# Layer B attention: where the rounding of the value differences and four output weight loads stand in their queues

## The chip, the core and the metric

The kernel runs on one core of one Trainium2 chip. The metric is the device time of one execution in microseconds (us). A core has a matrix engine, TensorE (PE in the profile; its weight loads are PEld), and three engines for elementwise work: VectorE (DVE), ScalarE (ACT) and GpSimd (POOL). SyncE (SP) issues the DMAs. Each engine works through its own list of instructions in order; semaphores hold an instruction back until what it needs is there. GpSimd does not touch the accumulator memory (PSUM) in this kernel; the other three do.

## The reference

A two-layer decoder trunk over one sequence of 2048 tokens of width 1024, in float32. Layer A is a causal attention with a forget gate over 16 heads of 64. Then keys and values for layer B are projected once for 4 shared heads. Layer B, which the change touches, is a sliding-window attention (window 128) in blocks of 128 queries; four query heads share one key/value head, and each head has a learned sink logit:

```
logits = einsum(q, k_band) * 64**-0.5          # k_band: the block before and the block's own keys
logits = where(in_window & valid, logits, -inf)
probs = softmax(concat([logits, sink]))[..., :-1]
out = einsum(probs, v_band)
h = h + (out * silu(gate)) @ w_out_b
```

## The kernel before

Every float32 operand of a matrix product is kept as a rounded high part and a remainder (tiles with `h` and `l`, or two halves of one tile), and a product is the sum of three or four matmuls of such parts.

The program is written with a framework that records operations and schedules them: it decides for each engine in which order its instructions stand, by dependencies and its own estimates. `self.tc.keep_in_program_order(ins)` pins an instruction behind the one that was recorded before it on the same engine, so that the scheduler cannot move it ahead.

Layer B's attention is the generator `attention_b` (L1308 on). Its units are the 64 pairs (block i of 16, key/value head g of 4). Step n of its loop does, in the order of the code:

- `scores(n)` (L1354 to L1373): eight matmuls into a PSUM tile, the mask (L1366), the sink (L1367) and the row maximum (L1370) on DVE, the exponentials on ACT (L1373, four of them, each followed by the read-out of its sum).
- `norm_weights(n-1)`: a reciprocal on DVE (L1382) and a product on POOL (L1383).
- `feed`: some matmuls of the output projection `project` (L1498), the filler between the parts of a step. A step gets 12 of them, in two groups of six. Two steps fill one PSUM bank (tag `pb`, one buffer), which DVE empties at the end (L1504) into the tile with the residual; SP then stores it (L1505).
- at n = 4i + 1, `differences(i)`: on POOL the value tile of block i less that of block i-1 (L1412), then high and low halves of the difference added (L1413).
- `weights_t(n-3)`: transposes on PE (L359), the high part on ACT (L1398), the remainder on DVE (L1399), and on POOL both times the triangle mask (L1402).
- `values(n-4)`: four matmuls (L1437), two with the values of block i-1 and two with the differences, a copy on ACT (L1444), two adds (L1447) and the gate (L1451) on DVE, and the result's high part on ACT (L1453) and remainder on DVE (L1454).
- at n = 4i + 2, `split_differences(i)`: the sum rounded on ACT (L1420), and the remainder as a last subtraction on POOL (L1421). The matmuls of step 4i + 4 and the three after it read the pair.
- loads for the next block on SP: queries and keys (L1327, L1328, L1331), values (L1340) and gates (L1344). L1331, for one, loads the keys' second copy, `big<-kb`.
- `weight_load(j)` for the numbers j in `B_WEIGHTS_AT[n]` (L85): 1 MB of the split output weights, `big<-wo` (L1476). Numbers 4 to 7 are read first by the projection in steps 10 and 11; two of them fill one tile, and the last tile comes free when earlier transposes are done with it.

Until step 7 the attention runs between the matmuls of the gate projection (L742); from step 8 on, the output projection fills. Steps then follow each other on PE without other work.

Of the kernel before, what the change touches and what calls it, by code (L numbers as in the profile page):

```python
# [18 lines left out]
ALU = mybir.AluOpType  # L19
# [10 lines left out]
HD = 64  # L30
# [51 lines left out]
B_AHEAD = 8  # L82
B_LOAD_AT = 6

B_WEIGHTS_AT = {4: (0,), 5: (1,), 6: (2,), 7: (3,), 8: (4, 5), 9: (6, 7)}  # L85
FEED_1 = 0
FEED_2 = 6

# [12 lines left out]
def f_(ap):  # L101
    return ap.bitcast(F32)
# [51 lines left out]
class Trunk:  # L154
# [1153 lines left out]
    def attention_b(self, res, dst):  # L1308

        nc, d = self.nc, self.d  # L1310
# [25 lines left out]
        def load_v(i):  # L1336

            ts_ = slice(i * P, (i + 1) * P)
            v = self.sb(("qn", "qn", "wr")[i % 3], [P, NKV, P], F32R)
            nc.sync.dma_start(  # L1340
                out=f_(v), in_=d["vb"][:, ts_, :].rearrange("g t e -> t g e")
            )
            g = yg[:, 2 + i % 2, :].rearrange("p (c t) -> p c t", t=P)
            nc.sync.dma_start(out=g, in_=d["gtb"][:, ts_].rearrange("(c p) t -> p c t", p=P))  # L1344
            blk[i][3:5] = v, g
# [70 lines left out]
        def split_differences(i):  # L1416

            t_ = dvs[i][:, :, :HD]
            dv = self.sb("wh", [P, NKV, P], F32R)
            nc.scalar.copy(dv[:, :, :HD], t_)  # L1420
            nc.gpsimd.tensor_tensor(dv[:, :, HD:], t_, f_(dv[:, :, :HD]), ALU.subtract)  # L1421
            dvs[i] = dv

        def values(u):
# [47 lines left out]
        def weight_load(j):  # L1472
            half, t = 1 - j // 4, j % 4 * 2
            if t % 4 == 0:
                W[half][t // 4] = self.sb("big", [P, 2, 4, CH], F32R)
            nc.sync.dma_start(  # L1476
                out=f_(W[half][t // 4][:, :, t % 4 : t % 4 + 2, :]),
                in_=d["wo"][half, t // 4, :, :, t % 4 : t % 4 + 2, :],
            )
# [37 lines left out]
        for n in range(N + V_LAG_B):  # L1517
            if n < N:
                scores(n)
            if 0 < n <= N:  # L1520
                norm_weights(n - 1)
            if n == T_LAG_B:
                php = self.sb("big", [P, 2, 2, 2, G, P], F32R)
            if n == V_LAG_B + NKV:
                odd += [[self.sb(t, [P, 4, P], F32R) for _ in range(2)] for t in ("wh", "wl")]
            o = (n - O_LAG_B) * per
            feed(o + FEED_1)
            if n % NKV == 1 and NKV < n < N:
                differences(n // NKV)
            if 0 <= n - T_LAG_B < N:  # L1530
                weights_t(n - T_LAG_B)
            feed(o + FEED_2)
            if 0 <= n - V_LAG_B < N:
                values(n - V_LAG_B)
            if n % NKV == 2 and NKV < n < N:
                split_differences(n // NKV)
            feed(o + per)
            if n < N:
                i, g = units[n]
                if g == NKV - 2 and i + 1 < NTB:  # L1540
                    load(i + 1)
                if g == NKV - 1 and i + 1 < NTB:
                    load_v(i + 1)
            for j in B_WEIGHTS_AT.get(n, ()):
                weight_load(j)
            yield
# [123 lines left out]
```

## Time and profile before

| what | before |
|---|---|
| median of 3 timed runs | 2434.48 us (2434.19 to 2435.48) |
| the profiled execution, its own time | 2432.39 us |
| its span, first to last instruction | 2430.3 us |
| granted TensorE clock over the span | 1.000 |
| busy in the span: PE, DVE, ACT, POOL | 99%, 71%, 52%, 41% |
| DMA | 436.04 MB, mean 179 GB/s |

In the rows of the profile, `L1420 ACT` is line 1420 on ScalarE, and `out<-in` names the tiles by the program's own names. A row of the waits says whose instruction stood idle for whom: total us, how often, the longest. In a timeline a row has its start, its length and, in brackets, the idle time just before it and who ended that. A row of windows has the stretch, its length, the busy us of PE, PEld, DVE, ACT and POOL, the clock, the busy share of the 16 DMA engines and GB/s. Starts are from the span's start; layer B's attention fills the stretch from some 2040 us to the end, with the output projection in it from 2109 us.

### The profile page before, as it was taken

Reading aid. Unit: us, or ns where it says so; the run is one execution under the profiler, and the core shown is the slowest. Engines: PE = TensorE matmul, PEld = TensorE weight load, DVE = VectorE, ACT = ScalarE, POOL = GpSimd, SP = SyncE. Lnnn points to the kernel's source line nnn. Section 1 sums busy time; section 2 is a strip of 40 time slices with the busy share of each in tenths; the row PEclk is TensorE's granted clock in tenths of the full one; section 3 lists DMA queues with packets and bytes.
Section 4 is the critical chain, followed back from the end, with each engine's and each line's share of the span. In section 5 each row is a group of like instructions: output and inputs, shape, how many; then the busy total and the mean of one; then the engine's idle time right before and its main releaser. Section 6 shows DMA issues by size and latency. Waiting matters only on the chain.

```text
span 2430.3 us, 36305 instructions
## 1 busy us (share of the span) xinstructions
PE 2405.9 (99%) x11960; PEld 2025.9 (83%) x11960; DVE 1729.5 (71%) x4086; ACT 1261.7 (52%) x2504; POOL 993.9 (41%) x642
## 2 busy tenths in 40 slices
PE   9999999999999999999999999999999999999999
PEld 7888899987888788888888878888888888888887
DVE  7656567735988888889988865556766543677775
ACT  5433324323878777777877761135323322455554
POOL 0000000011878777777878862200011000377775
PEclk9999999999999999999999999999999999999999
DMA  6656545677554655575466549965433574765552
GB/s 191 201 168 194 154 148 172 197 234 234 176 165 127 207 159 145 148 219 169 130 193 172 172 144 316 294 234 161 126 100 108 167 244 150 257 189 179 181 178 74
DMA packets 356989, 436.04 MB, mean 179 GB/s; under 512 B 65280, under 2 KB 248608, under 8 KB 350624
## 3 DMA queue, kind: packets, MB, share of 16 engines
q1 hardware_dynamic: 356800, 433.71, 59.0%
q8 instruction: 95, 1.56, 0.3%
q14 instruction: 94, 0.77, 0.1%
HBM read 273.69 MB, written 159.79 MB: 178 GB/s over the span
## 4 chain that ended last, share of the span: by engine, by line
PE 89%; DMA 4%; DVE 3%; ACT 2%; issue 1%; POOL 1%; SPq 0%; DVEq 0%; ACTq 0%; POOLq 0%
PE b L779 30%; PE pa L1044 10%; PE pb L1086 7%; PE pb L1498 5%; PE b L1271 5%; PE sc L1000 5%; PE sc L1001 5%; PE mx L955 5%; PE pb L742 3%; PE b L742 2%; PE pa L1437 2%; PE b L1354 2%; DMA wr<-wg 2%; PE pb L359 1%; PE pa L742 1%
## 5 line engine op out<-in xcount | busy, mean ns | idle before, releaser
L779 PE MATMUL b<-wh,big 128*128 128x512 f32 (+3 forms) x2560 | 771.4, 374 | 1.7 <-ACT wh L502 1.4
L1020 POOL TENSOR_TENSOR big<-st,big 128x1024 fp32r<-128x1024 f32 (+1 forms) x320 | 656.0, 2069 | 239.9 <-ACT big L1019 159.4
L779 PEld LDWEIGHTS b<-wh,big 128*128 128x128 f32 x2560 | 470.7, 188 | 73.5 <-ACT wh L502 3.9
L779 PE MATMUL b<-wl,big 128*128 128x512 f32 (+3 forms) x1280 | 473.6, 370 | 1.1 <-DVE wl L503 1.1
L1029 DVE TENSOR_TENSOR ac<-ac,st 128x512 f32<-128x512 f32 (+3 forms) x576 | 352.8, 612 | 52.1 <-ACT st L1016 26.6
L1016 ACT ACTIVATE st<-sc 128x512 f32<-128x512 f32 (+1 forms) x512 | 273.6, 582 | 119.7 <-PE sc L1001 52.3
L1044 PE MATMUL pa<-big 128*128 128x512 f32 (+3 forms) x1280 | 318.9, 365 | 0.6 <-POOL big L1020 0.6
L1019 ACT CAST big<-st 128x1024 fp32r<-128x1024 f32 (+1 forms) x320 | 295.5, 924 | 8.5
L779 PEld LDWEIGHTS b<-wl,big 128*128 128x128 f32 x1280 | 241.3, 189 | 36.8 <-DVE wl L503 4.6
L1044 PEld LDWEIGHTS pa<-big 128*128 128x128 f32 x1280 | 229.1, 190 | 38.8 <-POOL big L1020 2.1
L968 DVE TENSOR_REDUCE mt<-mx 128x1 f32<-128x384 f32 (+1 forms) x360 | 214.5, 598 | 30.4 <-PE mx L955 28.0
L511 ACT ACTIVATE sq<-b,r 128x512 f32<-128x512 f32 (+2 forms) x128 | 77.8, 608 | 302.7 <-PE b L779 302.7
L1000 PE MATMUL sc<-big 128*128 128x512 f32 (+3 forms) x640 | 232.9, 368 | 1.1 <-DVE st L558 1.1
L1001 PE MATMUL sc<-big 67*128 67x512 f32 (+3 forms) x640 | 229.5, 367 | 0.0
L955 PE MATMUL mx<-big 66*128 66x512 f32 (+2 forms) x600 | 225.0, 380 | 0.2
L1086 PE MATMUL pb<-wh,wr 128*128 128x512 f32 x488 | 177.7, 396 | 5.3 <-DMA wr<-wg 5.2
L513 DVE TENSOR_REDUCE sm<-sq 128x8 f32<-128x512 f32 (+2 forms) x128 | 74.8, 584 | 139.7 <-ACT sq L511 139.6
L1402 POOL TENSOR_TENSOR big<-big,tri 128x1024 fp32r<-128x1024 f32 x60 | 143.9, 2399 | 70.2 <-DVE big L1399 70.2
L879 POOL MEMSET rot<- 128x512 bf16 x1 | 0.5, 525 | 418.8 <-PE pb L359 418.8
L963 DVE CUSTOM_DVE_ANT_0 mx<-mx,rot 128x384 f32<-128x384 f32 (+2 forms) x240 | 146.9, 617 | 18.9 <-PE mx L955 17.6
L1000 PEld LDWEIGHTS sc<-big 128*128 128x128 f32 x640 | 121.7, 190 | 22.8 <-DVE st L558 1.5
L1001 PEld LDWEIGHTS sc<-big 67*128 67x128 f32 x640 | 121.8, 190 | 19.3
(285 smaller groups left out, 4122.1 us busy)
## 6 DMA issues: line engine op xcount, KB each, us to landing
wr<-wg SPq DMA_DIRECT2D x62, 512.0 KB, 4.5
va<-st SPq DMA_DIRECT2D x32, 512.0 KB, 4.6
ka<-st SPq DMA_DIRECT2D x64, 256.0 KB, 3.8
ut<-big SPq DMA_DIRECT2D x16, 1024.0 KB, 7.0
big<-ka SPq DMA_DIRECT2D x16, 1024.0 KB
big<-qa SPq DMA_DIRECT2D x16, 1024.0 KB, 8.1
qb<-st SPq DMA_DIRECT2D x64, 256.0 KB, 3.8
big<-qb SPq DMA_DIRECT2D x16, 1024.0 KB, 7.3
```

The source lines that it names most:

```text
L779: nc.tensor.matmul(ps[:, :n], u[tb // 4][:, dt, us], W[k][dt], start=(dt == 0 and i == 0), stop=(dt == NDT - 1 and i == 2),)
L955: mm = nc.tensor.matmul(ps, qb[:66, i * P : (i + 1) * P], kb[:66, k0:k1], start=True, stop=True,)
L963: nc.vector.tensor_tensor_reduce(out=ps, in0=ps, in1=mask_m[:, 512 - w :], scale=1.0, scalar=NEG, op0=ALU.add, op1=ALU.max, accum_out=f_(o),)
L968: nc.vector.reduce_max(o, ps, axis=AX.X)
L1000: nc.tensor.matmul(o, ka[:, ks], qa[:, qs], start=not (last and n_), stop=False)
L1001: nc.tensor.matmul(o, kb[:, ks], qb[:, qs], start=False, stop=not diag)
L1016: nc.scalar.activation(pf[:, off : off + w], ps[:, :w], AF.Exp, scale=HD**-0.5)
L1019: nc.scalar.copy(ph[:, :tw], pf[:, :tw])
L1020: nc.gpsimd.tensor_tensor(pl[:, :tw], pf[:, :tw], f_(ph[:, :tw]), ALU.subtract)
L1029: nc.vector.tensor_tensor(a_, a_, pf[:, off : off + w], ALU.add)
L1044: nc.tensor.matmul(pv[:, q0 : q0 + w], v[:, k, :], src[:, off : off + w], start=(p == 0 and n_ == 0 and i == 0), stop=(last and n_ == 1 an ...
L1086: nc.tensor.matmul(ps, w[:, dt // 2 % 2, wk, dt % 2, :], us[dt][uk], start=(dt == 0 and i == 0), stop=(dt == NDT - 1 and i == 2),)
```

## The change

In `split_differences` both instructions are pinned behind what was recorded before them on their engines, and the weight loads 6 and 7 are issued at step 8, with 4 and 5, instead of step 9.

```diff
-B_WEIGHTS_AT = {4: (0,), 5: (1,), 6: (2,), 7: (3,), 8: (4, 5), 9: (6, 7)}
+B_WEIGHTS_AT = {4: (0,), 5: (1,), 6: (2,), 7: (3,), 8: (4, 5, 6, 7)}
...
             dv = self.sb("wh", [P, NKV, P], F32R)
-            nc.scalar.copy(dv[:, :, :HD], t_)
-            nc.gpsimd.tensor_tensor(dv[:, :, HD:], t_, f_(dv[:, :, :HD]), ALU.subtract)
+            self.tc.keep_in_program_order(nc.scalar.copy(dv[:, :, :HD], t_))
+            self.tc.keep_in_program_order(
+                nc.gpsimd.tensor_tensor(dv[:, :, HD:], t_, f_(dv[:, :, :HD]), ALU.subtract)
+            )
             dvs[i] = dv
```

Behind these lines everything stands two lines lower: L1421 becomes L1422, L1453 becomes L1455, L1476 becomes L1478. The lists of PE and DVE keep their order; those of ACT, POOL and SP change.

On ACT, this stood before around the rounding of block 6 (`wl_22058` is the sum, `wh_22143` the rounded pair; `pa` tiles are units' outputs, `fl` tiles transposes; the time of this place is 2199.66 us in the trace):

```order
L1444 COPY wr_20470<-pa_22020 64x512 [waits PE_49,Activation_49]
L1373 ACTIVATE st_21996,rs_21994<-b2_21982,nm_21993 128x129 [waits DVE_49]
L1373 ACTIVATE st_21996,rs_21994<-b2_21982,nm_21993 128x129 x3
L1420 CAST wh_22143<-wl_22058 128x4x64 [waits Pool_49]
L1453 CAST wh_21073<-pa_22020 128x256 [waits DVE_49]
L1398 CAST big_20722<-fl_22061 128x512 [waits PE_49,Activation_49]
```

and this stands there now:

```order
L1455 CAST wh_21073<-pa_22020 128x256 [waits DVE_49]
L1398 CAST big_20722<-fl_22061 128x512 [waits PE_49,Pool_49]
L1373 ACTIVATE st_22051,rs_22049<-b2_22037,nm_22048 128x129 [waits DVE_49]
L1373 ACTIVATE st_22051,rs_22049<-b2_22037,nm_22048 128x129 x3
L1446 COPY wr_20470<-pa_22075 64x512 [waits PE_49,Activation_49]
L1398 CAST big_20722<-fl_22115 128x512 [waits PE_49,Pool_49]
L1455 CAST wh_21073<-pa_22075 128x256 [waits DVE_49]
L1446 COPY wr_20470<-pa_22132 64x512 [waits PE_49,Activation_49]
L1373 ACTIVATE st_22108,rs_22106<-b2_22094,nm_22105 128x129 [waits DVE_49]
L1373 ACTIVATE st_22108,rs_22106<-b2_22094,nm_22105 128x129 x3
L1455 CAST wh_21074<-pa_22132 128x256 [waits DVE_49]
L1420 CAST wh_22143<-wl_22058 128x4x64 [waits Pool_49]
```

The rounding L1420 has moved from ahead of the high part of `pa_22020` to behind that of `pa_22132`, two steps later (2209.6 us in the trace of before), where L1398 of the next transposes follows it.

On POOL, this stood before around the same block's differences:

```order
L1412 TENSOR_TENSOR wl_22058<-qn_21979,wr_21749 128x512 [waits DMAHW6_49]
L1413 TENSOR_TENSOR wl_22058<-wl_22058 128x4x64 [waits Pool_49]
L1383 TENSOR_TENSOR st_21939<-st_21939,rs_21937 128x4x128 [waits DVE_49]
L1421 TENSOR_TENSOR wh_22143<-wl_22058,wh_22143 128x4x64 [waits Activation_49]
L1402 TENSOR_TENSOR big_20722<-big_20722,tri_110 128x1024 [waits DVE_49]
```

and this stands there now:

```order
L1413 TENSOR_TENSOR wl_22058<-wl_22058 128x4x64 [waits Pool_49]
L1383 TENSOR_TENSOR st_21939<-st_21939,rs_21937 128x4x128 [waits DVE_49]
L1402 TENSOR_TENSOR big_20722<-big_20722,tri_110 128x1024 [waits DVE_49]
L1383 TENSOR_TENSOR st_21996<-st_21996,rs_21994 128x4x128 [waits DVE_49]
L1402 TENSOR_TENSOR big_20722<-big_20722,tri_110 128x1024 [waits DVE_49]
L1383 TENSOR_TENSOR st_22051<-st_22051,rs_22049 128x4x128 [waits DVE_49]
L1422 TENSOR_TENSOR wh_22143<-wl_22058,wh_22143 128x4x64 [waits Activation_49]
L1402 TENSOR_TENSOR big_20722<-big_20722,tri_110 128x1024 [waits DVE_49]
```

The last subtraction has moved past two mask products (L1402) and two weight products (L1383), and stands directly ahead of the third mask product.

On SP, this stood before around the last three of the eight weight loads (`big_21111` is the tile of loads 4 and 5, `big_21171` that of 6 and 7):

```order
L1476 DMA big_21111<-wo_73 128x2x1024 [waits DMAHW2_49]
L1476 DMA big_21171<-wo_73 128x2x1024 [waits DMAHW3_49,PE_49]
L1505 DMA out_h<-sq_21085 128x512 [waits DVE_49]
L1476 DMA big_21171<-wo_73 128x2x1024 [waits DMAHW5_49]
L1493 DMA sq_21203<-h1_68 128x512 [waits DMAHW6_49,DMAHW1_49]
L1331 DMA big_20666<-kb_70 64x4x256 [waits DMAHW7_49]
```

and this stands there now (`big_21114` is the tile of 6 and 7):

```order
L1478 DMA big_21111<-wo_73 128x2x1024 [waits DMAHW2_49]
L1478 DMA big_21114<-wo_73 128x2x1024 [waits DMAHW3_49,PE_49]
L1478 DMA big_21114<-wo_73 128x2x1024
L1507 DMA out_h<-sq_21085 128x512 [waits DMAHW5_49,DVE_49]
L1495 DMA sq_21203<-h1_68 128x512 [waits DMAHW6_49,DMAHW1_49]
L1331 DMA big_20666<-kb_70 64x4x256 [waits DMAHW7_49]
```

Only load 7 changes its place: from behind the first output store to ahead of it. Load 6 still waits for PE, which frees its tile.

## The prediction

> **What bounds the kernel now.** The page comes first. Its first line says that TensorE (PE) is busy nearly always, so a change pays only where PE stands still.
>
> ```profile
> PE 2405.9 (99%) x11960; PEld 2025.9 (83%) x11960; DVE 1729.5 (71%) x4086; ACT 1261.7 (52%) x2504; POOL 993.9 (41%) x642
> ```
>
> Next I read the waits of layer B's attention alone: first PE's own, from 1960 us on; then those of its weight loads (PEld) in the same stretch; then the weight loads between 2200 and 2380 us; then ScalarE's (ACT). Columns: total us, times, longest.
>
> ```profile
> PE pb L1498 <- DVE sq L1504: 2.8, 9, 0.5
> ```
>
> ```profile
> PEld pb L1498 <- DMA big<-wo: 2.1, 2, 1.6
> PEld b L1354 <- DMA big<-kb: 0.5, 1, 0.5
> PEld pa L1437 <- POOL big L1402: 0.3, 1, 0.3
> ```
>
> ```profile
> PEld pb L1498 <- DVE sq L1504: 5.0, 9, 0.7
> ```
>
> ```profile
> ACT wh L1420 <- POOL wl L1413: 21.9, 13, 2.2
> ```
>
> TensorE has three small leaks here. Nine times the output projection (L1498) waits for VectorE to empty its bank (L1504); two of the eight output weight loads come late (wo), and one load of keys (kb); once the values wait for GpSimd. The last row is no wait of TensorE, but it is the change's first target: ACT stands 21.9 us, in 13 places, in front of the rounding of the value differences, L1420.
>
> The rows 2.8 and 5.0 speak of the same nine waits. I take 5.0, because the starts bear it out: in the timeline of weight loads the projection's groups of six start at
>
> ```profile
> 2197.35 1.23 PEld L1498 LDWEIGHTS pb<-big 128*128 128x128 f32 x6
> ...
> 2202.93 1.22 PEld L1498 LDWEIGHTS pb<-big 128*128 128x128 f32 x6 [0.50 <-DVE sq L1504]
> ...
> 2207.98 1.23 PEld L1498 LDWEIGHTS pb<-big 128*128 128x128 f32 x6
> ```
>
> 5.58 us apart with the wait, 5.05 without: 0.53 for one, near 5.0 / 9 = 0.56, where 2.8 / 9 would be 0.31. With 2.8 in place of 5.0 the sum below would come out at 2431.6 us instead of 2429.4. The Trainium skill, page "Perfetto Trace Analysis", section "Identifying the Most-Contended Engine", calls the busy share of matmuls a poor measure, since they are pipelined, and prefers that of weight loads. The trace agrees with the page, by the 0.53.
>
> Is L1420 what makes L1504 late? The timelines of one such unit, POOL, ACT and DVE, show it (brackets: idle before, and who ended it):
>
> ```profile
> 2197.52 1.29 POOL L1412 TENSOR_TENSOR wl<-qn,wr 128x512 f32<-128x512 f32 x1
> 2198.89 0.74 POOL L1413 TENSOR_TENSOR wl<-wl 128x256 f32<-128x256 f32 x1
> ```
>
> ```profile
> 2199.66 0.41 ACT L1420 CAST wh<-wl 128x256 fp32r<-128x256 f32 x1 [1.70 <-POOL wl L1413]
> 2199.97 0.37 ACT L1453 CAST wh<-pa 128x256 fp32r<-128x256 f32 x1
> 2200.23 0.59 ACT L1398 CAST big<-fl 128x512 fp32r<-128x512 f32 x1
> ```
>
> ```profile
> 2197.38 0.43 DVE L1451 TENSOR_TENSOR pa<-pa,big 128x256 f32<-128x256 f32 x1
> ...
> 2200.37 0.43 DVE L1454 TENSOR_TENSOR wl<-pa,wh 128x256 fp32r<-128x256 f32 x1 [1.96 <-ACT wh L1453]
> ...
> 2200.93 0.69 DVE L1399 TENSOR_TENSOR big<-fl,big 128x512 fp32r<-128x512 f32 x1
> ...
> 2202.22 0.66 DVE L1504 TENSOR_TENSOR sq<-pb,sq 128x512 f32<-128x512 f32 x1
> ```
>
> L1453's input (L1451) was done at 2197.81, but L1453 ran at 2199.97, behind L1420, which waited for GpSimd's second subtraction to end at 2199.63. VectorE then stood 1.96 us for L1453, went through its list in order, ended L1504 at 2202.88, and TensorE went on at 2202.93. The wait is inherited from ACT's queue.
>
> **The change part by part.** *Rounding and last subtraction.* Nothing is added or removed; L1420 (0.41 us) goes two units down ACT's queue, behind the L1453 of its own step, and the third subtraction (L1421) follows on POOL. At the old place L1453 starts when ACT's exponentials end, at 2199.66 - 1.70 = 2197.96, instead of 2199.97, L1399 about 1.7 us sooner, and L1504 no longer waits for VectorE's list. What is late next there is shown by the unit two further on, which has no L1420 before and has the same emptying; it is the new place too. ACT, DVE, POOL and the weight loads there:
>
> ```profile
> 2209.33 0.37 ACT L1453 CAST wh<-pa 128x256 fp32r<-128x256 f32 x1
> 2209.60 0.59 ACT L1398 CAST big<-fl 128x512 fp32r<-128x512 f32 x1
> 2211.55 0.37 ACT L1373 ACTIVATE st<-b,nm 128x129 f32<-128x129 f32 x1 [1.36 <-DVE nm L1370]
> ```
>
> ```profile
> 2210.22 0.69 DVE L1399 TENSOR_TENSOR big<-fl,big 128x512 fp32r<-128x512 f32 x1
> ...
> 2211.43 0.17 DVE L1382 RECIPROCAL rs<-rs 128x4 f32<-128x4 f32 x1
> 2211.95 0.69 DVE L1504 TENSOR_TENSOR sq<-pb,sq 128x512 f32<-128x512 f32 x1 [0.35 <-PE pb L1498]
> ```
>
> ```profile
> 2208.99 1.04 POOL L1383 TENSOR_TENSOR st<-st,rs 128x512 f32<-128x512 f32 x1
> 2210.99 2.41 POOL L1402 TENSOR_TENSOR big<-big,tri 128x1024 fp32r<-128x1024 f32 x1 [0.96 <-DVE big L1399]
> ```
>
> ```profile
> 2213.03 0.30 PEld L1498 LDWEIGHTS pb<-big,wh 128*128 128x128 f32 x2
> ...
> 2214.77 0.42 PEld L1437 LDWEIGHTS pa<-big,wh 128*128 128x128 f32 x2
> ```
>
> VectorE waits here for TensorE (0.35), ends L1504 at 2212.64, and TensorE wants the bank at 2213.03: 0.39 to spare. So once the stall goes, the limit at the old place is TensorE itself. Gain: all nine, 5.0 us.
>
> At the new place the cost is this. L1413 ended ten us earlier, so L1420 waits for nothing; queued behind it stands L1398, which starts 0.31 later (two ACT instructions follow each other at that distance at 2199.66 and 2199.97). L1399 and L1382 move by 0.31 into the 0.35 that VectorE waits anyway; L1504 stays. On POOL the third subtraction (0.74, as L1413) runs in the 0.96 between 2210.03 and 2210.99, after L1420 ends at 2210.01; the mask product L1402 behind it starts 0.31 later, ends at 2213.71, and its readers on TensorE load weights from 2214.77: 1.1 to spare. ACT's delay passes on to its exponentials, but L1420 comes once in four units and L1504 every second, with 0.35 + 0.39 to spare each time, so it is taken up. Cost: nothing while those margins hold; without them up to 0.31 at each of the nine places, 2.8 us.
>
> The single wait of the values for POOL (0.3 on the weight loads, which run ahead) came with the last block, where the third subtraction stood ahead of the mask product and now stands behind it; I count 0.1.
>
> *The four weight loads.* No byte is added. The last load leaves SP's queue from behind the output store and goes right behind the third. SP around it before, from the chain of waits, and the weight loads that waited:
>
> ```profile
> 2118.70 0.34 SPq L1505
> ...
> 2119.10 0.53 SPq L1476
> ...
> 2120.33 9.83 DMA big<-kb
> ```
>
> ```profile
> 2121.80 1.22 PEld L1498 LDWEIGHTS pb<-big 128*128 128x128 f32 x6 [0.57 <-DMA big<-wo]
> ...
> 2128.28 1.23 PEld L1498 LDWEIGHTS pb<-big 128*128 128x128 f32 x6 [1.58 <-DMA big<-wo]
> ...
> 2130.21 0.89 PEld L1354 LDWEIGHTS b<-big 128*128 128x128 f32 x7 [0.47 <-DMA big<-kb]
> ```
>
> ```profile
> 2117.00:2127.00 10.00, 9.87 (x55) 8.02 (x53) 7.91 (x19) 5.76 (x22) 7.52 (x6) 1.00 1.04 401
> ```
>
> ```profile
> big<-wo SPq DMA_DIRECT2D x8, 1024.0 KB, 8.5
> ...
> out_h<-sq SPq DMA_DIRECT2D x32, 256.0 KB, 2.0
> ```
>
> ```profile
> SPq L1493 <- DMA out_h<-sq: 4.0, 1, 4.0
> ```
>
> The last weight load was issued at 2119.10, behind a store that waited for VectorE; now it can go as soon as the third has gone. That looks worth the 1.58. But from 2117 to 2127 the 16 DMA engines are full (share 1.04 in the row of the ten us, 401 GB/s), so an earlier issue only changes the order: the weights pass the store's 256 KB and land some 0.6 us sooner, while the keys, issued at 2120.33 and landed at 2130.16, have the same bytes ahead of them as before. TensorE loses less at 2126.7 and then waits longer for the keys. I count 0. At best nothing waits there any more, 1.58 + 0.47 = 2.05; at worst the keys lose what the weights win, 0.6. If the keys' landing went with their issue instead, 9.83 behind it and 0.53 sooner, the part would gain 0.5, and the sum would be 2428.9. The Trainium skill, page "DMA: Bandwidth & Descriptors", section "Queues, rings and completion order", says that on each DMA engine the descriptors of a ring are consumed in their order, which speaks against any gain from this part. By that rule 2429.4 stands; the trace agrees so far as the full ten us go, and only the changed kernel can show the rest.
>
> The store now lands later, behind 1 MB more: 2.6 us at 401 GB/s. One load of the residual waits for that landing (4.0 in the SP row), with block 4's values and queries behind it on SP. They are wanted four units of 5.05 after the keys, some 20 us, which covers 2.6; uncovered it would cost those 2.6 once.
>
> Sum against the profiled execution: 2432.39 - 5.0 - 0.1 - 0 = 2427.3. The timed runs have a median of 2434.48, 2.1 above it; the same 5.1 off gives 2429.4.
>
> **The rivals.** *The keys come sooner* (chance 0.15): the DMA part yields 0.5 to 2.05 as well, 2428.9 to 2427.3. For it: the chain runs through SP's issues. Against: the full engines.
>
> *The stall moves only, in part or whole* (0.24). Both places hold an emptying of the bank, and the new one has 0.35 + 0.39 to spare against 0.31. If those margins are thinner in other blocks, or L1504 has a second reason to be late, part comes back: 0.31 in nine places is 2.8, so 2432.2; if nothing is won, 2434.4, which is also the case where the change does not do what it says. Against: from L1413's end at 2199.63 to TensorE's start at 2202.93 each step of the list follows the one before it.
>
> *Slower: the third subtraction holds up GpSimd* (0.05). It now waits for ACT, in front of the mask product. If L1420 ends at T, the product ends at T + 0.05 + 0.74 + 2.41, and TensorE waits if that is past 2214.77: from T = 2211.57, where I expect 2210.01. If ACT ran 2.5 us late, each of the 12 blocks from the fourth on would lose 0.94: 2429.4 + 11.3 = 2440.7. Against: ACT has idle time (1.36) in that unit.
>
> *The forecast* has 0.56: 5.1 off, give or take 0.5.
>
> **How the numbers follow.** A difference under 0.2% (4.9 us) can hardly be told from none; so faster begins below 2429.6, and the forecast lies just inside it. I give it 0.39 of its 0.56 there, and with the 0.15 of the keys that makes 0.54; same takes the other 0.17 and the 0.24, 0.41; slower 0.05. The range goes from 2427.3 (keys at their best) to 2432.4 (the stall partly back), which leaves out slower and the case that nothing is won.
>
> **What would show it.** Right: the 5.0 of L1498 on L1504 is gone, L1420 has no idle time before it, L1504 waits 0.3 or more for TensorE in every such unit, the 1.58 shrinks and the 0.47 grows. Wrong: L1498 waits for L1504 at the units of the new place, L1437 waits for L1402, or ACT idles before another line as long as it did before L1420.

## The result, and the profile after

| | before | after |
|---|---|---|
| median of 13 timed runs each | 2432.51 us (2429.76 to 2436.95) | 2424.84 us (2422.77 to 2432.52) |
| the profiled execution, its own time | 2432.39 us | 2423.77 us |
| its span | 2430.3 us | 2421.8 us |

The ratio is 0.9973, with a 95% interval of 0.9965 to 0.998: faster by 6.6 us (4.9 to 8.5). The two medians lie 7.7 us apart; I go by the ratio, because the interval belongs to it. The forecast was 5.1 us off 2434.48, the median of the first three of these 13 runs of before; all 13 have 2432.51, 2.0 less. The median after lies 2.5 below the low end of the forecast's range. So the size to explain is 6.6 against 5.1, beside the 2.0 of the base.

First the busy line of the page after, then all waits of its weight loads from 1960 us to the end, the stretch in which the kernel before had the leaks that the prediction began with (columns: total us, times, longest).

```profile
PE 2403.3 (99%) x11960; PEld 2026.8 (84%) x11960; DVE 1732.2 (72%) x4086; ACT 1261.2 (52%) x2504; POOL 992.9 (41%) x642
```

```profile
PEld pb L742 <- ACT wh L502: 1.1, 1, 1.1
PEld pb L742 <- DVE sq L751: 0.7, 1, 0.7
PEld pb L1500 <- DVE sq L1506: 0.5, 2, 0.3
PEld pb L742 <- DVE wl L503: 0.5, 1, 0.5
```

The nine waits of 5.0 us are gone. So are all waits for DMA, 2.1 for the weights and 0.5 for the keys, and the 0.3 on the mask product. The two waits of L1500 that stay (0.5) are not of the nine: over the same stretch the row of before is

```profile
PEld pb L1498 <- DVE sq L1504: 5.5, 11, 0.7
```

and the L742 rows belong to the gate projection, which the change does not touch. On the other engines, the same stretch: VectorE's emptying of the bank before, and after; then GpSimd's third subtraction after.

```profile
DVE sq L1504 <- PE pb L1498: 19.0, 18, 4.7
```

```profile
DVE sq L1506 <- PE pb L1500: 49.8, 29, 4.7
POOL wh L1422 <- ACT wh L1420: 3.9, 15, 1.0
```

VectorE now waits for TensorE at 29 of the emptyings instead of 18, and the rounding L1420 has no row among ScalarE's waits any more. ScalarE's idle time has not gone, most of it has moved to a wait for TensorE's transposes, a row that was 9.2, 10, 2.8 before:

```profile
ACT big L1398 <- PE fl L359: 33.2, 42, 1.2
```

Here is the new place of the rounding in the timeline, on ScalarE, VectorE, GpSimd and the weight loads:

```profile
2204.18 0.37 ACT L1455 CAST wh<-pa 128x256 fp32r<-128x256 f32 x1
2204.45 0.41 ACT L1420 CAST wh<-wl 128x256 fp32r<-128x256 f32 x1
2204.75 0.59 ACT L1398 CAST big<-fl 128x512 fp32r<-128x512 f32 x1
...
2208.24 0.69 DVE L1506 TENSOR_TENSOR sq<-pb,sq 128x512 f32<-128x512 f32 x1 [1.49 <-PE pb L1500]
...
2204.93 0.74 POOL L1422 TENSOR_TENSOR wh<-wl,wh 128x256 fp32r<-128x256 f32 x1 [0.49 <-ACT wh L1420]
2206.14 2.40 POOL L1402 TENSOR_TENSOR big<-big,tri 128x1024 fp32r<-128x1024 f32 x1 [0.47 <-DVE big L1399]
...
2209.32 0.30 PEld L1500 LDWEIGHTS pb<-big,wh 128*128 128x128 f32 x2
```

The rounding costs L1398 behind it 0.30 (2204.75 - 2204.45). The third subtraction lies in time in which GpSimd waited anyway, and 0.47 of that is left. VectorE stands 1.49 before it can empty the bank, and ends 0.39 before TensorE wants it (2208.93, 2209.32).

Where did the time come from? The output projection runs from its first matmul to its last through nearly the whole stretch that the change touches. These are the two ends, before and after:

```profile
2108.96 1.64 PE L1498 MATMUL pb<-big 128*128 128x512 f32 x6
...
2425.64 0.39 PE L1498 MATMUL pb<-big,wl 128*128 128x512 f32 x1
```

```profile
2108.02 1.64 PE L1500 MATMUL pb<-big 128*128 128x512 f32 x6
...
2417.23 0.39 PE L1500 MATMUL pb<-big,wl 128*128 128x512 f32 x1
```

316.68 and 309.21 us: 7.5 of the 8.6 between the two profiled executions. 0.94 of the rest is the earlier start. One rounding, that of the first differences, moves ahead of this start (from 2012.9 to 2097.5), but the start doesn't follow the order: in the runs it falls from 2106.80 to 2111.14 with the old order and from 2106.88 to 2110.34 with the new one. So I compare this stretch and not the spans.

### The profile page after: what moved, and what is told of

Its sections match the earlier page's. It is cut to its first block, busy times and chain, and to the rows that moved or that the text cites. A ratio compares the mean times of both kernels' runs of the same rounds, so it can differ in the third digit from the quotient of the medians.

```text
span 2421.8 us, 36285 instructions
## 1 busy us (share of the span) xinstructions
PE 2403.3 (99%) x11960; PEld 2026.8 (84%) x11960; DVE 1732.2 (72%) x4086; ACT 1261.2 (52%) x2504; POOL 992.9 (41%) x642
## 3 DMA queue, kind: packets, MB, share of 16 engines
q1 hardware_dynamic: 356800, 433.71, 59.1%
## 4 chain that ended last, share of the span: by engine, by line
PE 92%; DMA 4%; DVE 2%; ACT 1%; issue 1%; POOL 0%; SPq 0%; ACTq 0%; POOLq 0%; DVEq 0%
PE b L779 31%; PE pa L1044 10%; PE pb L1086 7%; PE pb L1500 7%; PE sc L1000 5%; PE sc L1001 5%; PE mx L955 5%; PE b L1271 4%; PE pb L742 3%; PE b L1354 3%; PE pa L1439 2%; PE b L742 2%; DMA wr<-wg 1%; PE fl L359 1%; PE pb L359 1%; PE pa L742 1%
## 5 line engine op out<-in xcount | busy, mean ns | idle before, releaser
L968 DVE TENSOR_REDUCE mt<-mx 128x1 f32<-128x384 f32 (+1 forms) x360 | 214.1, 597 | 30.6 <-PE mx L955 28.5
L1402 POOL TENSOR_TENSOR big<-big,tri 128x1024 fp32r<-128x1024 f32 x60 | 144.2, 2403 | 59.1 <-DVE big L1399 59.1
L1000 PEld LDWEIGHTS sc<-big 128*128 128x128 f32 x640 | 121.6, 190 | 22.8 <-DVE st L558 1.5
```

The lines of the kernel that those rows point to most:

```text
L968: nc.vector.reduce_max(o, ps, axis=AX.X)
L1000: nc.tensor.matmul(o, ka[:, ks], qa[:, qs], start=not (last and n_), stop=False)
```

## The experiments

Two explanations of the 6.6 stood against each other, and a third beside them. The theory on record: the order of the rounding is worth about 5, the loads nothing. Rival A: the loads' new place gains as well. Rival B: how late weights and keys come differs from run to run, whatever the order. The first eight kernels ran beside the kernel before in two groups, whose medians of before were 2430.49 (29 runs) and 2432.63 (22 runs). Each group had a chip of its own, so I compare ratios from group to group, and times only within a group.

**The order alone (twice).** The loads stay where they were; the edit on the kernel before is the second hunk of the change:

```diff
-            nc.scalar.copy(dv[:, :, :HD], t_)
-            nc.gpsimd.tensor_tensor(dv[:, :, HD:], t_, f_(dv[:, :, :HD]), ALU.subtract)
+            self.tc.keep_in_program_order(nc.scalar.copy(dv[:, :, :HD], t_))
+            self.tc.keep_in_program_order(
+                nc.gpsimd.tensor_tensor(dv[:, :, HD:], t_, f_(dv[:, :, :HD]), ALU.subtract)
+            )
```

> The rounding and the third subtraction are held in order; the four weight loads stay where they were before. Theory on record (the nine waits cost 5.0 us, the loads 0): 5.1 us under the kernel before, as much as the whole change; in the trace no L1498 waits for L1506, and output weights or keys still come late by about 2 us at the start of the attention. Rival A (the loads' new place gained the rest): 5.1 us under before, but the whole change lies a further 1.6 to 2.5 us below this kernel, and the late weights and keys are here and not in the whole change. Rival B (how late the weights and keys come differs from run to run, whatever the order): this kernel equals the whole change within the measurement, and its trace may show any lateness from 0 to 3 us.

> The order of the rounding and the subtraction alone, the loads where they were, once more. First time: ratio 0.9985 to the kernel before, 1.5 us of late weights and keys in its trace. If the order alone is worth the 5.1 us of the record, the ratio comes nearer to 0.9979; if it is worth the 3.6 of the first time, the loads' new place is needed for the 6.6 of the whole. If the lateness of the weights and keys belongs to the old place of the loads, it is there again (1.5 to 2.6 us); if it differs from run to run, it may be anything from 0 to 3.

Measured: 2426.14 and 2426.86 us, ratios 0.9985 (0.9976 to 0.9993) and 0.9975 (0.9967 to 0.9984); on average 0.998, 4.9 us. The weight loads' waits for the output projection and the keys, first run and second:

```profile
PEld pb L1500 <- DMA big<-wo: 1.1, 1, 1.1
PEld pb L1500 <- DVE sq L1506: 0.5, 2, 0.3
PEld b L1354 <- DMA big<-kb: 0.4, 1, 0.4
```

```profile
PEld pb L1500 <- DMA big<-wo: 2.1, 2, 1.6
...
PEld b L1354 <- DMA big<-kb: 0.4, 1, 0.4
```

The nine waits go with the order alone, and the lateness of weights and keys stays. The second ratio is no worse than that of the whole change (0.9973), so these times alone do not show that the loads' place is worth anything.

**The loads alone (twice).** The other half of the change. On SP the last of the four loads goes ahead of the output store; no other instruction moves.

```diff
-B_WEIGHTS_AT = {4: (0,), 5: (1,), 6: (2,), 7: (3,), 8: (4, 5), 9: (6, 7)}
+B_WEIGHTS_AT = {4: (0,), 5: (1,), 6: (2,), 7: (3,), 8: (4, 5, 6, 7)}
```

> Only the four weight loads are put in one place; the rounding and the subtraction stay free. Theory on record (the DMA engines are full, an earlier issue only changes the order): no change of time, 0 +- 0.6 us; in the trace the last weight load comes about 1 us late instead of 1.6 and the keys about 1 us instead of 0.5; the nine waits of 5.0 us stay. Rival A (landing follows the issue): 1.6 to 2.5 us faster, no weight and no keys late. Rival B (the lateness differs from run to run): within 1 us of before, with any lateness from 0 to 3 us in the trace.

> The loads in one place alone, once more. First time: ratio 0.9992, no late weights or keys. If landing follows the issue: again 1.6 to 2.5 us faster, and the keys' bulk lands within 5.2 us of that of the third of the four loads (6.2 at the old place in the kernel with the order alone). If the lateness differs from run to run: about 0 us, lateness from 0 to 3, and the distance from the third load to the keys like that of the old place.

Measured: 2428.42 and 2430.57 us, ratios 0.9992 (0.9983 to 1.0001) and 0.9993 (0.9984 to 1.0002): about 1.8 us each time, with no change just inside either interval. The traces tell more than the times. The first run's weight loads have no wait for DMA in the attention, the second run's have these, and the waits for the emptying stay (4.7):

```profile
PEld pb L1498 <- DVE sq L1504: 4.7, 11, 0.6
...
PEld b L1354 <- DMA big<-kb: 0.4, 1, 0.4
PEld pb L1498 <- DMA big<-wo: 0.4, 1, 0.4
```

**The third subtraction alone held in order.**

```diff
-            nc.gpsimd.tensor_tensor(dv[:, :, HD:], t_, f_(dv[:, :, :HD]), ALU.subtract)
+            self.tc.keep_in_program_order(
+                nc.gpsimd.tensor_tensor(dv[:, :, HD:], t_, f_(dv[:, :, :HD]), ALU.subtract)
+            )
```

> Only the third subtraction is held in order; the rounding L1420 stays free, and so stays at its old place on ScalarE, right behind GpSimd's second subtraction; the loads stay as before. Theory (VectorE and TensorE inherit the wait of the rounding on ScalarE): nothing is won, 0 +- 0.5 us, L1420 waits some 22 us for L1413 in 13 places and the nine waits of 5.0 us stay. Rival (GpSimd's list was what made the emptying late, since the third subtraction stood ahead of the mask product): about 5 us faster, and the nine waits go although L1420 still waits.

Measured: 2429.95 us, ratio 1.0006 (0.9995 to 1.0016). ScalarE's row and the weight loads':

```profile
ACT wh L1420 <- POOL wl L1413: 21.8, 13, 2.2
```

```profile
PEld pb L1500 <- DVE sq L1506: 4.8, 11, 0.6
```

Nothing is won, and both rows are nearly those of before (21.9 and 5.5). So the gain of the order hangs on the rounding's place on ScalarE; the rounding held without the subtraction was not run. The small wait of the values for the mask product (0.3) is not there, so this half of the pinning does take that away.

**The whole change once more, beside its parts.** No edit.

> The whole change once more, on the same chip as its parts. Theory on record: equal to the kernel with the order alone (5.1 us under before). Rival A (the loads' new place gains as well): 1.6 to 2.5 us below the kernel with the order alone, and no weight or key comes late in this second profile either. Rival B (the lateness differs from run to run): within 1 us of the kernel with the order alone, and this second profile may show late weights or keys, from 0 to 3 us.

Measured: 2423.59 us, ratio 0.9975 (0.9964 to 0.9986): 6.1 us, near the sum of the parts (4.9 + 1.8), and 2.6 us below the order alone in the same group (2426.14), as Rival A would have it. But weights and keys came late in this profile:

```profile
PEld pb L1500 <- DMA big<-wo: 1.9, 2, 1.2
...
PEld b L1354 <- DMA big<-kb: 0.3, 1, 0.3
```

So the lateness is not simply abolished by the new place; Rival B is partly right.

**A dose on GpSimd.** A second, smaller subtraction ahead of the first one of the differences makes the sum later; its result is overwritten by the full one. The same edit on the kernel before and on the whole change:

```diff
+            nc.gpsimd.tensor_tensor(
+                t[:, :, :HD], v[:, :, :HD], before[:, :, :HD], ALU.subtract
+            )
```

> The kernel before, with one subtraction of 128x256 more (about 0.74 us, its result is overwritten by the full one) ahead of GpSimd's first subtraction of the value differences. Theory (TensorE inherits, through ScalarE's queue and VectorE's list, the wait of the rounding for GpSimd): the rounding waits at least 0.74 us longer in its 13 places, and the nine emptyings of the output projection come at least that much later: 9 x 0.74 = 6.7 us slower, up to 16 where GpSimd's rescaling of the values (1.04) also comes in between. Rival (the emptying is late by VectorE's own list, and the rounding's wait only stands beside it): no change, 0 to 1 us.

Measured on the kernel before: 2453.5 us, ratio 1.0087 (1.0072 to 1.0102): 21 us slower, above the bound of 16. The line numbers behind the edit are three higher here. ScalarE's wait at the rounding, 21.9 before, and one unit in the timeline, on GpSimd, ScalarE, VectorE and the weight loads:

```profile
ACT wh L1423 <- POOL wl L1416: 40.8, 13, 3.4
```

```profile
2205.37 1.04 POOL L1383 TENSOR_TENSOR st<-st,rs 128x512 f32<-128x512 f32 x1
2206.37 0.74 POOL L1416 TENSOR_TENSOR wl<-wl 128x256 f32<-128x256 f32 x1
...
2207.62 0.73 POOL L1424 TENSOR_TENSOR wh<-wl,wh 128x256 fp32r<-128x256 f32 x1 [0.52 <-ACT wh L1423]
2209.18 2.37 POOL L1402 TENSOR_TENSOR big<-big,tri 128x1024 fp32r<-128x1024 f32 x1 [0.82 <-DVE big L1399]
...
2207.14 0.41 ACT L1423 CAST wh<-wl 128x256 fp32r<-128x256 f32 x1 [3.38 <-POOL wl L1416]
...
2207.85 0.42 DVE L1457 TENSOR_TENSOR wl<-pa,wh 128x256 fp32r<-128x256 f32 x1 [3.63 <-ACT wh L1456]
...
2209.21 0.42 PEld L359 LDWEIGHTS fl<-ident,st 128*128 128x128 f32 x4 [1.37 <-POOL wh L1424]
2210.41 1.53 PEld L1501 LDWEIGHTS pb<-big 128*128 128x128 f32 x6 [0.78 <-DVE sq L1507]
```

The chain is the forecast's, link by link, and it is longer now: GpSimd's sum (an addition, which the prediction calls the second subtraction), the rounding, the high part behind it on ScalarE, VectorE's list. The dose is larger than its 0.74: the framework has also put the product L1383 (1.04) ahead of the sum, behind which it stood before, and the rounding waits 3.38 in this unit instead of 1.70. But a second victim comes ahead of the projection. The transposes L359 need the PSUM tile `fl` that VectorE's L1399 in the same list has yet to empty; TensorE's own row has 11 such waits and names L1399. The weight loads' row names the third subtraction, L1424, but that had ended at 2208.35, 0.86 before the transposes; L1399 ended just ahead of 2209.18, where GpSimd's mask product, which waits for it too, started.

```profile
PE fl L359 <- DVE big L1399: 10.4, 11, 1.4
```

```profile
PEld fl L359 <- POOL wh L1424: 11.2, 8, 1.6
PEld pb L1501 <- DVE sq L1507: 9.1, 13, 0.8
PEld pb L1501 <- DMA big<-wo: 1.8, 1, 1.8
...
PEld fl L359 <- issue: 1.1, 3, 0.4
PEld b L1354 <- DMA big<-kb: 0.9, 1, 0.9
```

These five rows are 24.1 us, where the kernel before has 8.4 (5.5 + 2.1 + 0.5 + 0.3): 15.7 more. The rest is the clock. Windows behind three of the stalls (the clock is the column ahead of the last two):

```profile
2211.00:2215.00 4.00, 4.00 (x12) 3.17 (x11) 3.09 (x8) 1.99 (x6) 2.44 (x3) 0.57 0.39 133
...
2323.00:2327.00 4.00, 3.80 (x10) 2.99 (x11) 2.45 (x7) 2.19 (x8) 2.44 (x3) 0.61 0.32 116
...
2391.00:2396.00 5.00, 4.61 (x13) 3.67 (x14) 3.45 (x9) 2.99 (x12) 3.44 (x3) 0.66 0.31 108
```

4 x 0.43 + 4 x 0.39 + 5 x 0.34 = 5.0 us of clock not granted. Together 20.7; the projection's stretch is 21.1 longer than in the profile of before (337.74 against 316.68).

> The whole change, with the same extra subtraction on GpSimd. Theory (behind the unit's values the rounding waits for nothing, and the mask product has 1.1 us to spare): the same time as the whole change, 0 to 1 us above it, and ScalarE's rounding still without a wait. Rival (GpSimd's list is as near to the bound as ScalarE's was, and the third subtraction in front of the mask product passes the delay on): 0.74 x 12 = 9 us above the whole change, with TensorE's values waiting for the mask product.

Measured on the whole change: 2425.34 us, ratio 0.9969 (0.9958 to 0.9981), where the change without the dose has 0.9973 and 0.9975. L1383 has gone ahead of the sum here too, and the rounding has no row among ScalarE's waits. The time of the dose comes out of GpSimd's waits for the mask product; without the dose the row is 59.1, with it

```profile
POOL big L1402 <- DVE big L1399: 49.2, 44, 3.9
```

The same edit, 0.74 us of work and the 1.04 that it put ahead of the sum, cost 21 us at one place of the rounding and nothing that can be measured at the other.

**The first of the four loads earlier still.** The edit on the whole change:

```diff
-B_WEIGHTS_AT = {4: (0,), 5: (1,), 6: (2,), 7: (3,), 8: (4, 5, 6, 7)}
+B_WEIGHTS_AT = {4: (0,), 5: (1,), 6: (2,), 7: (3, 4), 8: (5, 6, 7)}
```

> The whole change, and the first of the four loads one unit earlier still (with the one of the unit before), so that on SP it goes ahead of the load of the residual, which waits there 1.7 us for a store to land. If lateness of weights and keys is what the new place of the loads takes away, and goes with the time of issue: the first load is issued about 1.7 us sooner after the start of layer B's attention than 8.0, all four land sooner by up to that, no weight load waits any more, and the time falls by what is left of the lateness in the profiles of the whole change (0, 2.2 and 0.6 us): 0 to 1 us. If the full queue only changes its order: the residual's 256 KB change places with 1 MB of weights, the keys land as before, 0 us, and the late residual may cost up to 2 us where the first emptyings of the output projection wait for it.

Measured beside the kernel before (2432.93): 2427.75 us, ratio 0.9979 (0.997 to 0.9989): no better than the whole change. The load was issued 1.6 us sooner after the attention's first load of keys (6.4 against 8.0) but had half of its 16 completions only at 14.4, where the same load has them from 14.5 to 15.3 in the other three profiles with the whole change. Here, where other loads were still ahead of it, an earlier issue moved the landing little. The residual, now behind that load, came late, as the forecast feared: its last completion was at 2116.87, VectorE's first emptying began at 2116.95, 0.85 after TensorE had filled the bank, and TensorE waited 0.5 for it.

**What the ten profiles say together.** For each: the projection's stretch, first matmul to last; the weight loads' waits in it for DMA (weights and keys) and for VectorE's emptying, from rows like those above; what is left of the stretch without both; then, in us after the issue of the attention's first load of keys (L1328, `big<-kb`, near 2100 us), when the third and the last of the four weight loads and the second copy of the keys were there: the median of the 16 completions of each DMA, and for the last load and the keys the last one too.

| kernel | stretch | DMA | emptying | left | third | last load | its last | keys | their last |
|---|---|---|---|---|---|---|---|---|---|
| before | 316.68 | 2.6 | 5.5 | 308.6 | 21.0 | 24.2 | 26.9 | 26.4 | 28.8 |
| subtraction alone | 315.63 | 2.0 | 4.8 | 308.8 | 19.8 | 23.7 | 26.3 | 26.0 | 28.4 |
| order alone | 310.56 | 1.5 | 0.5 | 308.6 | 19.9 | 23.8 | 26.0 | 26.1 | 27.9 |
| order alone, again | 311.33 | 2.5 | 0.5 | 308.3 | 20.9 | 24.0 | 26.8 | 26.3 | 28.7 |
| loads alone | 314.33 | 0 | 5.3 | 309.0 | 19.7 | 22.2 | 22.8 | 24.9 | 25.6 |
| loads alone, again | 314.70 | 0.8 | 4.7 | 309.2 | 20.6 | 23.1 | 25.3 | 25.7 | 27.2 |
| whole change | 309.21 | 0 | 0.5 | 308.7 | 20.2 | 22.7 | 24.4 | 25.5 | 26.5 |
| whole change, again | 311.11 | 2.2 | 0.5 | 308.4 | 20.9 | 23.4 | 26.7 | 26.0 | 28.5 |
| whole change, dose | 309.56 | 0.6 | 0.5 | 308.5 | 20.0 | 22.6 | 25.1 | 25.2 | 26.9 |
| fourth load earlier | 310.05 | 0.5 | 1.0 | 308.6 | 20.7 | 23.2 | 25.9 | 25.9 | 27.3 |

The two kinds of wait account for nearly all of the difference: what is left is 308.3 to 309.2, and 308.3 to 308.8 when the values' wait for the mask product (0.3 before, 0.3 and 0.6 with the loads alone) is taken off as well. The emptying costs 4.7 to 5.5 with the rounding at its old place and 0.5 at the new one (1.0 in the last row): 4.6 us. The DMA costs 1.5 to 2.6 with the loads at the old place (2.7 in the dose on before), 2.3 on average of five, and 0 to 2.2 at the new one, 0.7 on average of six: 1.6 us, of which 1.2 are waits for weights (1.7 against 0.5) and 0.4 waits for the keys (0.6 against 0.2). One new run, the whole change again, reaches into the old ones.

What TensorE waits for is the last of the 16 completions: wherever it waited for the last load, it began within 0.05 us of that load's "its last". It wants those weights at 24.9, where no earlier wait has held it up. That last completion came at 26.0 to 26.9 with the loads at the old place and at 22.8 to 26.7 at the new one, 1.5 us sooner on average; 1.0 of this is in the medians (23.9 and 22.9), the rest is that the slowest engine lagged less behind them.

Why the keys can land sooner with the same bytes ahead shows in windows of 2 us, with the order alone and then with the loads alone (last two columns: busy share of the DMA engines, GB/s):

```profile
2118.00:2120.00 2.00, 2.00 (x10) 1.62 (x9) 2.00 (x7) 0.70 (x2) 1.16 (x1) 1.00 1.03 387
2120.00:2122.00 2.00, 2.00 (x16) 1.84 (x15) 1.46 (x6) 1.98 (x11) 2.00 (x2) 1.00 1.01 317
2122.00:2124.00 2.00, 2.00 (x12) 1.68 (x10) 1.99 (x5) 0.95 (x3) 1.17 (x3) 1.00 0.99 319
```

```profile
2120.00:2122.00 2.00, 2.00 (x10) 1.63 (x10) 1.78 (x6) 1.57 (x5) 2.00 (x1) 1.00 1.02 420
2122.00:2124.00 2.00, 2.00 (x17) 1.87 (x16) 1.68 (x5) 1.95 (x9) 1.80 (x3) 1.00 1.03 391
```

The busy share says full in all five, but at the old place the rate falls from 387 to 317 GB/s as soon as the third load is through. The last load is issued 17.7 after the start there, and its median completion came 6.0 to 6.5 later in all five profiles with the old place; none of the four loads was ever faster from issue to landing, by that median. So where the third was through by 20 (three of the five, the dose on before among them), it seems that the last could not follow it at full rate. In the profile of before, and in the order alone again, the third load came late enough (21.0 and 20.9) to hide that: the rate held, and the prediction saw a full queue. So this is not the whole cause: these two have DMA waits of 2.6 and 2.5 without any fall of the rate. And where the third load came as late with the new place (20.9, the whole change again), 2.2 of waits stayed, not far from what the prediction expected of a full queue. The Trainium skill, page "Perfetto Trace Analysis", section "Identifying the Most-Contended Engine", advises to judge DMA by its throughput, because the occupancy of 16 engines misleads. The five rows agree with it: the share is 0.99 to 1.03 in all of them, the rate 317 to 420.

## Why the prediction was right about the rounding and wrong about the loads

- **The nine waits, 5.0.** Right in mechanism, near in size: the nine are gone, 4.6 on average of the profiles and 4.9 by the timed order alone. That the wait was inherited from ScalarE's queue is shown from three sides: holding only the subtraction leaves it, holding the rounding as well removes it, and a later sum makes it longer.
- **What is late next.** "The limit at the old place is TensorE itself": right, VectorE waits for it at 29 emptyings. At the new place I foresaw L1398 0.31 later and got 0.30, and 0.39 to spare at the bank and got 0.39. I foresaw VectorE waiting 0.35 there, and it is 1.49: without the stall two steps earlier the whole list runs further ahead, so the margins grew where I took them as given. One of the signs that I had named for being wrong did appear, ScalarE idle before another line as long as before L1420: 24.0 us more before L1398. It was a bad sign to name: L1398 waits there for TensorE itself, the engine that bounds this stretch, and no wait of TensorE leads back to it.
- **The third subtraction in front of the mask product.** It cost nothing, as foreseen: TensorE has no wait for the mask product after the change, and even the dose on GpSimd cost nothing there. The rival "slower" did not come true.
- **The values' wait, 0.1.** It went; the weight loads' row was 0.3, and the time cannot tell such a size.
- **The four loads, "I count 0".** This is the step that failed. "An earlier issue only changes the order" and "TensorE loses less at 2126.7 and then waits longer for the keys": I set 0.6 won by the weights against 0.6 lost by the keys. The waits for weights fell by 1.2, and those for keys did not grow but fell by 0.4. The keys came sooner too, by 0.7 us on average of the medians (25.5 in six profiles against 26.2 in four) and 1.4 by their last completion (27.0 against 28.4). The bytes ahead were the same, but in three of five profiles the engines were not kept at full rate for them at the old place, and the last completions lagged less at the new one. The rule that I took from the Trainium skill ("DMA: Bandwidth & Descriptors", "Queues, rings and completion order"), descriptors consumed in order, is not contradicted by that: it says in which order, not at what rate, and I had read the one for the other. I had put this outcome among the rivals at 0.5 to 2.05 us with a chance of 0.15; measured are 1.6 by the waits and 1.8 by the times, though the interval of either time still just contains no effect. The later landing of the store was covered, as foreseen: it landed 1.4 later (25.0 against 23.6 after the first load of keys, where I had 2.6), and TensorE waited for nothing behind it.
- **The base.** Forecast and range hung on a median of three runs, 2434.48. This step failed too: all 13 runs have 2432.51, near the profiled 2432.39 that I had set aside, and the later groups 2430.49 to 2432.93. Of the 4.6 us between 2429.4 and 2424.84, 2.0 are this base and no effect of the change, 1.5 are the gain that I had too small (6.6 against 5.1), and 1.1 are the difference between the ratio and the two medians. From 2432.51 my range would have begun at 2425.3, still 0.5 above the measured median.

With 1.6 in place of 0 the sum would have been 6.7 us, against 6.6 measured. That it fits so closely is in part luck: with 4.6 in place of the 5.0 it is 6.3, and the interval of the 6.6 goes from 4.9 to 8.5.

Still open: the last completions. At the old place the slowest of the 16 DMA engines ended the keys 1.7 to 2.7 us behind the median, at the new one 0.7 to 2.5, and no run tells why some engines lag or why the whole change, run again, lagged by 2.5. It is also open whether the smaller lag comes from the loads' new place or differs by chance from run to run, and the fall of the rate was seen, not made. A kernel with the four loads in smaller pieces might tell them apart; it wasn't tried.

## What to carry to other kernels

When an engine waits in front of an instruction that nobody needs soon, look at what stands behind it in its queue: here 21.9 us of ScalarE's waiting reached TensorE as 5, through an instruction that had nothing to do with the one that waited. A DMA queue that looks full in one profile need not be full in the next run: look at its GB/s in short windows, and at the last of its completions, in several profiles before counting an earlier issue at nothing. And compare the stretch that the change touches, first to last instruction, since its start alone moved by 4 us between runs.

## What the runs showed of the hardware

The granted clock fell after short stalls. In the dose on the kernel before, TensorE stood 1.37 and 0.78 us within 3 us (the weight loads' rows above); then the clock went to half for about 3.4 us. These are single microseconds around the end of one such stall:

```profile
2210.00:2211.00 1.00, 0.59 (x3) 0.49 (x4) 0.36 (x1) 1.00 (x7) 1.00 (x1) 1.00 0.04 8
2211.00:2212.00 1.00, 1.00 (x4) 0.80 (x3) 0.12 (x1) 0.95 (x4) 1.00 (x2) 0.64 0.69 258
2212.00:2213.00 1.00, 1.00 (x4) 0.78 (x3) 0.97 (x3) 0.46 (x1) 0.54 (x1) 0.50 0.01 4
```

It did so behind three of eight stalls of that size; behind the others, for one the stall that ended at 2186.8 us, the clock stayed at 1.00. The Trainium skill, page "TensorE: Matmul & The Clock Gate", part 1, says that the clock is halved after an idle window of some 3.4 us, and that these windows run freely. The length of the slow stretch fits that, and so does it that only some stalls were hit; but here no such idle time was longer than 1.6 us. In the profiles of before and after the clock is 1.00 all through the attention, so the 6.6 us hold nothing of it; but a change that makes such stalls can pay for them nearly twice: 2.15 us of standing at that place, and 1.7 of clock not granted.
